# Mixer of a three-block transformer: five more convolution taps on Pool, the forget gates' chain called later in the code, a head's output copied out of PSUM by ScalarE

## The chip, the cores and the metric

The kernel runs on one core of a Trainium2 chip, in one launch. The metric is the device time of an execution in microseconds; the time of the kernel before is the median of three runs, 2093.25 us (2092.4 to 2098.12). One more execution was recorded by the hardware profiler; that one took 2092.26 us.

## The reference, cut to what matters

512 tokens of width 1024 go through two transformer blocks (differential attention, then windowed attention, each with a gated MLP and a gated side input) and then through the block that the change touches, the mixer:

```python
def conformer_conv_branch(a_in, w_dw, b_dw, g_ln, b_ln, w_out):
    a = a_in[..., :CONV_CH] * jax.nn.sigmoid(a_in[..., CONV_CH:])   # 512 channels
    a = causal_depthwise_conv(a, w_dw, b_dw)                        # 31 taps
    a = jax.nn.silu(layernorm(a, g_ln, b_ln))
    return a @ w_out

def forgetting_attention(q, k, v, f_logit, b_forget, g_q, g_k):     # 8 heads of 64
    ...  # rmsnorm of q and k in each head
    log_f = jax.nn.log_sigmoid(f_logit + b_forget)
    c = jnp.cumsum(log_f, axis=1)
    ...  # softmax(q k / 8 + c_i - c_j), causal, times v

proj = rmsnorm(x, g_mix) @ w_in     # a_in, q, k, v, f_logit, gate_a, gate_b
merged = sigmoid(gate_a) * y_conv + sigmoid(gate_b) * (y_attn @ w_attn_out)
x = x + merged @ w_out              # then one more gated MLP
```

## The kernel before, in words

All activations lie feature-major, as tiles of 128 features by 512 tokens. Every matrix product keeps f32 accuracy by splitting both operands into a high and a low part and adding three products (`mm3`, L188 to L190): high by high, high by low, low by high. So each 512 KB block of weights arrives by DMA (`wr`), is cast by ScalarE (`wh`, L157), and its low part is made by VectorE (`wl`, L158). A `dense` output of 128 features costs 24 matmuls of 128x512 (8 weight blocks, three products each).

The mixer (`mix`) has four tiles of 128 convolution channels, m = 0 to 3. `glu(m)` makes the convolution's input `pad` and the running sum `cacc`. `tap(m, j, ...)` adds tap j of tile m. For the tiles 0 and 1 the first `VT[m]` taps run on VectorE, multiply and add in one instruction into `pacc` in PSUM (L918), and the others on Pool: a product `tap` (made by Pool itself while the attention runs, L924, or by ScalarE afterwards, L926) and Pool's add into `cacc` (L927). With VT = (31, 20), tile 0 is all VectorE's, and of tile 1 twenty taps are VectorE's and eleven are Pool's. The tiles 2 and 3 are all Pool's.

The attention: `qk(m)` projects a pair of heads' k and q; `unit_heads` normalises each of the two by `inv_rms`: squares `isq`, high and low part `ish` and `isl` (L416, L417), a sum over each head's 64 rows by two matmuls into `ps_ss` (L418, L419), and from that the factor `iy` (L425). Eight such halves are made, two of them ahead of the heads. `head(hd)` makes `nb` (the row of -c, L1009 and L1011), four score blocks with their softmax, four transposed blocks (`ps_t`, L1039) split into `ah` and `al`, and twelve matmuls into `ps_o` (L188 to L190, of 512, 384, 256 and 128 columns, three each); the last step splits `ps_o` into the high and low output `xq` (L180 on ScalarE, L181 on VectorE). This text calls the part from the transposes on a head's tail. Between the score blocks the other projections (`gens`) and the taps (`taps`) are called.

After the attention come 16 `gate` products `w_g`, with the remaining taps called between the first twelve, then `attn_conv` of `w_ao` over the attention, and `conv_norm`: `cs`, the sum over the four finished tiles (L1100 on Pool, L1101 and L1102 on VectorE), its split `csh`, the mean over channels by `ps_cs` (L1114), the centred squares, the variance (`ps_tm`, `ps_bc`, L217), SiLU, and the split `cxh`, the operand of `w_co`.

Tiles with one tag of one pool form a ring: in the pool `fp` each tag has three buffers unless told otherwise. Tag "A" holds `nb`, `u` (a projection before its normalisation), `ish` and later `cs`; tag "C" holds `isq`, `isl`, `iy`, `tap` and `csh`. A tile that takes a buffer waits for the last reader of the tile that had it before.

The order of the instructions on each engine is not the code's: the tile framework reorders the program as a list scheduler (`schedule_with_timeline_sim=True`), by dependencies, ring buffers and a model of durations, except where `keep` holds the order of the code. So an edit moves instructions at places that the diff doesn't touch.

Of the kernel before, what the change touches and what calls it, by code (L numbers as in the profile page):

```python
# [11 lines left out]
F32 = mybir.dt.float32  # L12
F32R = mybir.dt.float32r
I32 = mybir.dt.int32
AF = mybir.ActivationFunctionType
ALU = mybir.AluOpType
# [3 lines left out]
P = 128  # L20
D = 1024
T = 512
# [23 lines left out]
SSP = (4, 5)  # L46


VT = (31, 20)
TAPS = ((0, 1),) * 5 + ((0, 2),) * 3  # L50
CSTEP = 12

# [39 lines left out]
def build(tc, nc, a, out):  # L92
    c = Ctx()
# [5 lines left out]
    fp = es.enter_context(tc.tile_pool(name="fp", bufs=3))  # L99
# [5 lines left out]
    V, S, G, TE, Q = nc.vector, nc.scalar, nc.gpsimd, nc.tensor, nc.sync  # L105
# [17 lines left out]
    def spc(name, i=0, n=1):  # L123
        o, w = _SP[name]
        return sp[:, o + i : o + i + n]
# [10 lines left out]
    def act(**kw):  # L136

        name = SETS[kw["func"]]
        if aset["name"] != name:
            ld = S.preload_act_table_set(name)  # L140
            if aset["name"] == LNEXP:
                tc.keep_in_program_order(ld)
            for u in aset["users"]:
                tc.add_manual_dep(ld.ins, u, nosync, reason="tables in order")
            aset.update(name=name, load=ld.ins.name, users=[])
        i = S.activation(**kw)  # L146
        tc.add_manual_dep(i.ins, aset["load"], nosync, reason="tables in order")
        aset["users"].append(i.ins.name)
# [29 lines left out]
    def split(hi, lo, src, scale=None):  # L178
        if scale is None:
            S.copy(out=hi, in_=src)  # L180
            V.tensor_tensor(out=lo, in0=src, in1=rd(hi), op=ALU.subtract)  # L181
        else:
            S.activation(out=hi, in_=src, func=AF.Copy, scale=scale)
            V.scalar_tensor_tensor(out=lo, in0=src, scalar=scale, in1=rd(hi), op0=ALU.mult, op1=ALU.subtract)  # L184
# [45 lines left out]
    h = [None] * KD  # L230
# [630 lines left out]
    def mix(nm, nxt):  # L861
# [25 lines left out]
        def glu(m):  # L887
            pad = mp.tile([P, NT - 1 + T], F32, tag="cv", name="pad", bufs=8)
            G.memset(pad[:, 0 : NT - 1], 0.0)
            V.tensor_tensor(out=pad[:, NT - 1 :], in0=dense("w_a", 2 * m, x), in1=nm.rb, op=ALU.mult)  # L890
            pads[m] = pad
            yield
            u = mp.tile([P, T], F32, tag="cv", name="cacc", bufs=8)
            V.tensor_tensor(out=u, in0=dense("w_a", 2 * m + 1, x), in1=nm.rb, op=ALU.mult)
            accs[m] = u
            yield

        def glu_gate(m):
# [3 lines left out]
            V.scalar_tensor_tensor(out=p, in0=u, scalar=1.0, in1=p, op0=ALU.add, op1=ALU.mult)  # L902
            n = VT[m] if m < 2 else 0
            bgv.extend((m, j, V) for j in range(n))
# [41 lines left out]
        V.tensor_tensor(out=lg, in0=psf, in1=nm.rb[0:8, :], op=ALU.mult)  # L946
        fq, y, z, w = (sm.tile([P, 32], F32, tag="f" + n, name="f" + n, bufs=1) for n in "qyzw")
        Q.dma_start(out=fq, in_=lg.rearrange("h (c t) -> h c t", t=32))
        V.tensor_scalar(out=fq, in0=fq, scalar1=spc("bf"), scalar2=None, op0=ALU.add)
        V.scalar_tensor_tensor(out=y, in0=fq, scalar=-1.0, in1=fq, op0=ALU.mult, op1=ALU.min)  # L950
        act(out=y, in_=y, func=AF.Exp)

        V.tensor_scalar(out=z, in0=y, scalar1=2.0, scalar2=None, op0=ALU.add)
        V.reciprocal(out=z, in_=z)
        V.tensor_tensor(out=z, in0=z, in1=y, op=ALU.mult)
        V.tensor_tensor(out=w, in0=z, in1=z, op=ALU.mult)
        V.tensor_scalar(out=y, in0=w, scalar1=2.0 / 17.0, scalar2=2.0 / 15.0, op0=ALU.mult, op1=ALU.add)
        for n in (13, 11, 9, 7, 5, 3, 1):
            V.tensor_tensor(out=y, in0=y, in1=w, op=ALU.mult)
            V.tensor_scalar(out=y, in0=y, scalar1=2.0 / n, scalar2=None, op0=ALU.add)  # L960
        V.tensor_tensor(out=y, in0=y, in1=z, op=ALU.mult)
        V.scalar_tensor_tensor(out=y, in0=fq, scalar=0.0, in1=y, op0=ALU.min, op1=ALU.subtract)
        lf = fp.tile([8, T], F32, tag="B", name="lf", bufs=4)
        Q.dma_start(out=lf.rearrange("h (c t) -> h c t", t=32), in_=y)
        cc = fp.tile([8, T], F32, tag="B", name="cc", bufs=4)
        V.tensor_tensor_scan(out=cc, data0=lf, data1=lf, initial=0.0, op0=ALU.add, op1=ALU.bypass)
        ch = ma.tile([P, T], F32R, name="ch")
        G.memset(ch.bitcast(I32), 0)
        split(ch[0:8], ch[32:40], cc)

        def unit_heads(ps, g, tag, bufs):

# [11 lines left out]
        def qk(m):  # L984

            pk = dense("w_qk2", 2 * m + 1, x)
            hk = unit_heads(pk, gqk[:, 1:2], "hk", 1)
            yield
            pq = dense("w_qk2", 2 * m, x)
            hq = unit_heads(pq, gqk[:, 0:1], "hq", 1)  # L990
            yield
            for j in range(2):
                sl = slice(64 * j, 64 * j + 64)
                q, k, kl = (ma.tile([P, T], F32R, tag="st", name="st", bufs=9) for _ in range(3))
                for b in range(2):
                    o = slice(64 * b, 64 * b + 64)
                    Q.dma_start(out=rd(k[o]), in_=rd(hk[sl, 0]))
                    Q.dma_start(out=rd(q[o]), in_=rd(hq[sl, b]))
                    Q.dma_start(out=rd(kl[o]), in_=rd(hk[sl, 1]))
                sts[2 * m + j] = q, k, kl  # L1000
            yield

        ox = Quads()

        def head(hd):
            q, kh, kl = sts[hd]

            pc = att.tile([P, T], F32, tag="tp", name="ps_c")
            TE.matmul(pc, nid[:, hd : hd + 1].to_broadcast([P, P]), ch, start=True, stop=True)  # L1009
            nb = fp.tile([P, T], F32, tag="A", name="nb")  # L1010
            S.copy(out=nb, in_=pc)  # L1011
            ee = []
            for i in range(4):
                wd = (i + 1) * P
                ps = att.tile([P, T], F32, tag="sc", name="ps_s", bufs=BANKS["sc"])
                scores(ps[:, :wd], q, kh, kl, slice(i * P, wd), slice(0, wd), False)
                TE.matmul(ps[:, i * P : wd], idr, trir, start=False, stop=True)
                mx = sm.tile([P, 1], F32, tag="mx", name="mx")
                su = sm.tile([P, 1], F32, tag="su", name="su")
                if i < 2:  # L1020
                    e = ma.tile([P, 256], F32, tag="e", name="e", bufs=3)
                else:
                    e = fp.tile([P, T], F32, tag="B", name="e", bufs=4)
                V.tensor_tensor_reduce(
                    out=e[:, :wd], in0=ps[:, :wd], in1=nb[:, :wd], scale=1.0, scalar=-3.0e38,
                    op0=ALU.add, op1=ALU.max, accum_out=mx,
                )
                V.tensor_scalar(out=mx, in0=mx, scalar1=-1.0, scalar2=None, op0=ALU.mult)
                act(out=e[:, :wd], in_=e[:, :wd], func=AF.Exp, bias=mx, scale=1.0, accum_out=su)
                V.reciprocal(out=su, in_=su)  # L1030
                V.tensor_scalar(out=e[:, :wd], in0=e[:, :wd], scalar1=su, scalar2=None, op0=ALU.mult)
                ee.append(e)
                yield
            po = att.tile([64, T], F32, tag="po", name="ps_o", bufs=1)
            for kb in range(4):
                wd = T - kb * P
                pt = att.tile([P, T], F32, tag="tp", name="ps_t")
                for i in range(kb, 4):
                    TE.transpose(pt[:, (i - kb) * P : (i - kb + 1) * P], ee[i][:, kb * P : (kb + 1) * P], ident)  # L1039
                ah, al = (ma.tile([P, T], F32R, tag=n, name=n, bufs=2) for n in ("ah", "al"))  # L1040
                split(ah[:, :wd], al[:, :wd], pt[:, :wd])
                vb = tuple(z[:, hd * 64 : hd * 64 + 64] for z in vt[kb])
                mm3(po[:, kb * P :], vb, (ah[:, :wd], al[:, :wd]), kb == 0, kb == 3)
            par = slice((hd % 2) * 64, (hd % 2) * 64 + 64)
            split(*(z[par] for z in ox[hd // 2]), po)
            yield


# [3 lines left out]
        def vproj(hf):  # L1052
            pss = tok_major("w_v2", 2 * hf, x)
            cols = slice(256 * hf, 256 * hf + 256)
            for t in range(4):
                split(vt[t][0][:, cols], vt[t][1][:, cols], pss[t], nm.rt[:, t : t + 1])
            yield

        for _ in chain(qk(0), vproj(0), *(glu(m) for m in (2, 3))):
            pass  # L1060
        for m in (2, 3):
            glu_gate(m)
# [106 lines left out]
        for m in range(KD):  # L1169
            t = ga[m]  # L1170
# [168 lines left out]
```

## Time and profile before

| what | us |
| --- | --- |
| median of three runs | 2093.25 (2092.4 to 2098.12) |
| the profiled execution | 2092.26 |
| its span, first to last instruction | 2090.3 |
| TensorE (PE) busy | 2007.4 |
| VectorE (DVE) busy | 1374.4 |
| ScalarE (ACT) busy | 908.1 |
| Pool busy | 472.4 |

The mean granted clock of TensorE is 0.987 of full speed. The mixer fills about 1301 to 1700 us of the span, its attention about 1400 to 1565, and the taps end at 1631. A busy time counts overlapped matmuls once; a wait is idle time of an engine with the instruction that ended it. PE is TensorE, DVE VectorE, ACT ScalarE.

### The profile page before, as it was taken

The numbers are of one execution on the slowest core, as the hardware profiler recorded it, in microseconds if no ns is written. First come the engines' busy times: TensorE is split into PE (matmuls) and PEld (weight loads), VectorE is DVE, ScalarE is ACT, GpSimd is POOL, SyncE is SP. The second block draws the span as 40 slices with busy tenths as digits, with TensorE's granted clock in tenths as the row PEclk, the third lists the DMA queues.
The fourth block names the chain that finished last, engine by engine and source line by source line (L and its number), as shares of the span: only waits on it lengthen the run. The fifth ranks groups of instructions, "written<-read, shape, count | busy, mean of one in ns | idle before, by whom it ended". The sixth has DMA issues, their size and how long they took to land.

```text
span 2090.3 us, 25027 instructions
## 1 busy us (share of the span) xinstructions
PE 2007.4 (96%) x9374; PEld 1650.3 (79%) x9374; DVE 1374.4 (66%) x2174; ACT 908.1 (43%) x1447; POOL 472.4 (23%) x337
## 2 busy tenths in 40 slices
PE   7999889999999998989999999999999899999999
PEld 6888668888888876768888888778778688888887
DVE  7786858747466756777647467778889765434443
ACT  5465635424244536654324244545556343222221
POOL 2465322000002236530000002305599040000000
PEclk9999999999999999999999999999999999999999
DMA  4643422232223252212222223233222232222222
GB/s 162 170 122 104 149 71 91 81 110 101 92 101 125 106 172 72 81 51 92 89 103 101 93 99 133 75 100 119 86 86 73 79 106 96 93 99 101 91 101 91
DMA packets 69465, 212.43 MB, mean 102 GB/s; under 512 B 9568, under 2 KB 9568, under 8 KB 68832
## 3 DMA queue, kind: packets, MB, share of 16 engines
q1 hardware_dynamic: 69344, 210.84, 30.3%
q8 instruction: 74, 1.21, 0.2%
q14 instruction: 47, 0.39, 0.1%
HBM read 179.31 MB, written 6.29 MB: 89 GB/s over the span
## 4 chain that ended last, share of the span: by engine, by line
PE 78%; DVE 10%; POOL 5%; ACT 3%; issue 2%; DMA 2%; SPq 0%; POOLq 0%; DVEq 0%; ACTq 0%
PE ps_d L188 24%; PE ps_d L190 24%; PE ps_d L189 24%; POOL cacc L927 3%; DVE wl L158 1%; POOL tap L924 1%; DMA wr<-w_qk 1%; PE ps_s L395 1%; PE ps_s L396 1%; PE ps_o L189 1%; PE ps_o L190 1%; ACT e L146 1%; PE ps_o L188 1%; ACT wh L157 1%; DVE xV L184 1%
## 5 line engine op out<-in xcount | busy, mean ns | idle before, releaser
L157 ACT CAST wh<-wr 128x1024 fp32r<-128x1024 f32 (+1 forms) x323 | 337.8, 1048 | 650.3 <-PE ps_d L189 563.5
L188 PE MATMUL ps_d<-xO,wh 128*128 128x512 f32 x1400 | 548.3, 392 | 7.2 <-ACT wh L157 3.3
L190 PE MATMUL ps_d<-xO,wl 128*128 128x512 f32 (+1 forms) x1400 | 547.9, 392 | 3.6 <-DVE wl L158 3.6
L189 PE MATMUL ps_d<-xV,wh 128*128 128x512 f32 (+1 forms) x1400 | 547.0, 391 | 0.0
L158 DVE TENSOR_TENSOR wl<-wr,wh 128x1024 fp32r<-128x1024 f32 x286 | 367.3, 1286 | 83.3 <-ACT wh L157 81.1
L188 PEld LDWEIGHTS ps_d<-xO,wh 128*128 128x128 f32 x1400 | 263.0, 188 | 65.3 <-ACT wh L157 5.4
L190 PEld LDWEIGHTS ps_d<-xO,wl 128*128 128x128 f32 (+1 forms) x1400 | 262.8, 188 | 60.4 <-DVE wl L158 5.3
L189 PEld LDWEIGHTS ps_d<-xV,wh 128*128 128x128 f32 (+1 forms) x1400 | 262.9, 188 | 55.8 <-DVE xV L184 0.6
L271 POOL TENSOR_TENSOR ss<-ss,sq 128x512 f32<-128x512 f32 x44 | 69.6, 1582 | 800.4 <-ACT sq L269 787.8
L314 DVE TENSOR_TENSOR u<-ps_d,rb 128x512 f32<-128x512 f32 x156 | 106.4, 688 | 203.5 <-PE ps_d L190 196.4
L189 PE MATMUL ps_d<-gl,wh 128*128 128x512 f32 x528 | 204.4, 389 | 0.0
L190 PE MATMUL ps_d<-gh,wl 128*128 128x512 f32 x528 | 203.2, 389 | 0.0
L188 PE MATMUL ps_d<-gh,wh 128*128 128x512 f32 x528 | 203.2, 389 | 0.0
L188 PE MATMUL ps_d<-xq,wh 128*128 128x512 f32 x448 | 179.1, 404 | 21.2 <-ACT wh L157 8.7
L190 PE MATMUL ps_d<-xq,wl 128*128 128x512 f32 x448 | 178.6, 399 | 1.4 <-DVE wl L158 1.3
L189 PE MATMUL ps_d<-xq,wh 128*128 128x512 f32 x448 | 178.8, 399 | 0.9 <-DVE xq L184 0.9
L766 DVE TENSOR_TENSOR h<-h,ps_d 128x512 f32<-128x512 f32 x72 | 48.6, 685 | 175.4 <-PE ps_d L190 175.4
L188 PEld LDWEIGHTS ps_d<-xq,wh 128*128 128x128 f32 x448 | 86.3, 193 | 40.9 <-ACT wh L157 9.0
L158 POOL TENSOR_TENSOR wl<-wr,wh 128x1024 fp32r<-128x1024 f32 x37 | 90.5, 2451 | 111.0 <-ACT wh L157 95.7
L189 PEld LDWEIGHTS ps_d<-gl,wh 128*128 128x128 f32 x528 | 99.1, 188 | 20.7
L188 PEld LDWEIGHTS ps_d<-gh,wh 128*128 128x128 f32 x528 | 99.1, 188 | 20.6
L190 PEld LDWEIGHTS ps_d<-gh,wl 128*128 128x128 f32 x528 | 99.2, 188 | 20.4
(317 smaller groups left out, 3127.5 us busy)
## 6 DMA issues: line engine op xcount, KB each, us to landing
wr<-w_up SPq DMA_DIRECT2D x132, 512.0 KB, 3.4
wr<-w_dn SPq DMA_DIRECT2D x66, 512.0 KB, 3.5
wr<-w_qk SPq DMA_DIRECT2D x34, 512.0 KB, 3.5
qst<-rt SPq DMA_DIRECT2D x64, 128.0 KB, 2.7
wr<-w_pg SPq DMA_DIRECT2D x16, 512.0 KB, 3.5
wr<-w_g SPq DMA_DIRECT2D x16, 512.0 KB, 3.4
wr<-w_v SPq DMA_DIRECT2D x14, 512.0 KB, 3.5
st<-qhl SPq DMA_DIRECT2D x48, 128.0 KB, 2.3
```

Of the source, the lines that this page charges most:

```text
L146: i = S.activation(**kw)
L157: S.copy(out=hi, in_=raw)
L158: lo_eng[0].tensor_tensor(out=lo, in0=raw, in1=rd(hi), op=ALU.subtract)
L184: V.scalar_tensor_tensor(out=lo, in0=src, scalar=scale, in1=rd(hi), op0=ALU.mult, op1=ALU.subtract)
L188: TE.matmul(ps, lh, rh, start=start, stop=False)
L189: TE.matmul(ps, lh, rl, start=False, stop=False)
L190: TE.matmul(ps, ll, rh, start=False, stop=stop)
L271: (V if self.first and k not in SSP else G).tensor_tensor(out=self.ss, in0=self.ss, in1=sq, op=ALU.add)
L314: V.tensor_tensor(out=u, in0=ps, in1=rb, op=ALU.mult)
L395: TE.matmul(ps, q[:, qc], k[:, kc], start=True, stop=False)
L766: V.tensor_tensor(out=h[m], in0=h[m], in1=ps, op=ALU.add)
L927: G.tensor_tensor(out=accs[m], in0=accs[m], in1=t, op=ALU.add)
```

## The change

Three edits in `mix`. `VT` goes from (31, 20) to (31, 15), so that tile 1 has five `L918` less on VectorE and five products on ScalarE with five adds on Pool more. The forget gates' chain, from the bias to the split of `ch`, becomes a function that is called behind the first `qk` and `vproj` in the code. And a head's output is copied from PSUM into a tile `ou` by ScalarE, and the split reads `ou`; `ou` is a tile of tag "A", in the ring of three with `nb`, `u` and `ish`.

```diff
-VT = (31, 20)
+VT = (31, 15)
@@
-        V.tensor_scalar(out=fq, in0=fq, scalar1=spc("bf"), scalar2=None, op0=ALU.add)
...
-        split(ch[0:8], ch[32:40], cc)
+
+        def forget():
+
+            V.tensor_scalar(out=fq, in0=fq, scalar1=spc("bf"), scalar2=None, op0=ALU.add)
...
+            split(ch[0:8], ch[32:40], cc)
@@
             par = slice((hd % 2) * 64, (hd % 2) * 64 + 64)
-            split(*(z[par] for z in ox[hd // 2]), po)
+            u = fp.tile([P, T], F32, tag="A", name="ou")[par]
+            S.copy(out=u, in_=po)
+            split(*(z[par] for z in ox[hd // 2]), u)
@@
-        for _ in chain(qk(0), vproj(0), *(glu(m) for m in (2, 3))):
+        for _ in chain(qk(0), vproj(0)):
+            pass
+        forget()
+        for _ in chain(*(glu(m) for m in (2, 3))):
             pass
```

Behind the edits the lines of the changed kernel are counted 3 higher in `head` and 8 higher from the gates on (L1012 for L1009, L1042 for L1039, L1122 for L1114).

ScalarE, around the `ish` of the last of the eight halves. Before, head 3's `ps_o` is cast straight into `xq`, two instructions ahead of the squares:

```order
L146 ACTIVATE e,su<-e,mx 128x512
L183 ACTIVATE qhl<-u,gs 128x512
L180 CAST xq<-ps_o 64x512
L1011 COPY nb<-ps_c 128x512
L413 ACTIVATE isq<-u 128x512
L416 CAST ish<-isq 128x512
L157 CAST wh<-wr 128x1024
```

In the changed kernel:

```order
L180 CAST ah<-ps_t 128x256
L180 CAST ah<-ps_t 128x128
L1049 COPY ou<-ps_o 64x512
L180 CAST xq<-ou 64x512
L413 ACTIVATE isq<-u 128x512
L416 CAST ish<-isq 128x512
L157 CAST wh<-wr 128x1024
L1014 COPY nb<-ps_c 128x512
```

The head is now head 4, one further, and its last transposed blocks, its copy and its cast stand ahead of `ish`. `ish` takes the buffer of tag "A" that `ou` of this head has, and so waits for VectorE's subtraction that reads it. The same holds for three other of the last six halves, behind the heads 0, 1 and 3.

TensorE, at the last half's two sums. Before, they stand between blocks of the convolution's projection and ahead of head 4's first `ps_o`:

```order
L189 MATMUL ps_d<-xV,wh 128x512
L418 MATMUL ps_ss<-ish,blkr 128x512
L395 MATMUL ps_s<-st 128x256
L396 MATMUL ps_s<-st 128x256
L1017 MATMUL ps_s<-trir,idr 128x128
L395 MATMUL ps_s<-st 128x384
L419 MATMUL ps_ss<-isl,blkr 128x512
L396 MATMUL ps_s<-st 128x384
L188 MATMUL ps_o<-ah,xq 64x512
```

In the changed kernel the tail of head 4 stands 23 matmuls of `ps_d` ahead of the first of them; its end is this:

```order
L188 MATMUL ps_o<-ah,xq 64x384
L1042 MATMUL ps_t<-cn,e 128x128
L189 MATMUL ps_o<-al,xq 64x384
L190 MATMUL ps_o<-ah,xq 64x384
L1042 MATMUL ps_t<-cn,e 128x128 x2
L188 MATMUL ps_o<-ah,xq 64x256
L189 MATMUL ps_o<-al,xq 64x256
L190 MATMUL ps_o<-ah,xq 64x256
L188 MATMUL ps_o<-ah,xq 64x128
L1012 MATMUL ps_c<-ch,nid 128x512
L189 MATMUL ps_o<-al,xq 64x128
L190 MATMUL ps_o<-ah,xq 64x128
```

From the mixer's start to the last L419, the changed order has thirty 128x512 matmuls of `ps_d`, the twelve of a head's `ps_o`, one `ps_c` and four `ps_t` more than the order before, and two score blocks (256 and 384 columns) and one 128-column mask less. For the six halves among the heads the whole difference up to their L419 is, in columns of 512, about 0, 32, 23, 16, 7 and 38.

Pool, at the end of the taps. Before:

```order
L924 TENSOR_TENSOR tap<-pad,dwh 128x512
L927 TENSOR_TENSOR cacc<-cacc,tap 128x512 x20
L1100 TENSOR_TENSOR cs<-cacc 128x512
L927 TENSOR_TENSOR cacc<-cacc,tap 128x512 x9
L1100 TENSOR_TENSOR cs<-csq 128x512
```

In the changed kernel:

```order
L924 TENSOR_TENSOR tap<-pad,dwh 128x512
L927 TENSOR_TENSOR cacc<-cacc,tap 128x512 x21
L1108 TENSOR_TENSOR cs<-cacc 128x512
L927 TENSOR_TENSOR cacc<-cacc,tap 128x512 x13
L1108 TENSOR_TENSOR cs<-csq 128x512
```

Five adds more stand ahead of the end. Of the 32 times three matmuls of `w_ao`, 16 single ones stand ahead of `ps_cs` in the changed kernel where 30 did, and 29 instead of 14 between `ps_tm` and `ps_bc`. The products that Pool makes itself (L924) are as many as before, and the first of the last run of them waits for the sixth L419 in both orders. The forget gates' instructions keep their places on every engine: VectorE's order is the same, but for line numbers, far into the attention.

## Rows read from the trace of the kernel before

**Rows 1.** The page: busy time of each engine, share of the span, instructions.

```profile
PE 2007.4 (96%) x9374; PEld 1650.3 (79%) x9374; DVE 1374.4 (66%) x2174; ACT 908.1 (43%) x1447; POOL 472.4 (23%) x337
```

**Rows 2.** What TensorE waited for in 1360 to 1700 us (the mixer): engine, matmul, what ended the wait; us in total, times, longest.

```profile
PE ps_d L188 <- ACT cxh L180: 3.3, 1, 3.3
...
PE ps_cs L1114 <- ACT csh L180: 2.9, 1, 2.9
PE ps_o L189 <- DVE al L181: 2.6, 2, 2.3
```

**Rows 3.** TensorE in order of time at the end of the convolution: start, duration, line, what, and the idle time before it with what ended it. The first two rows are the first and last of 27 matmuls that follow one another.

```profile
1624.61 0.39 PE L188 MATMUL ps_d<-xq,wh 128*128 128x512 f32 x1
...
1630.53 0.39 PE L190 MATMUL ps_d<-xq,wl 128*128 128x512 f32 x1
1633.78 0.50 PE L1114 MATMUL ps_cs<-csh,onesr 128*128 128x512 f32 x1 [2.87 <-ACT csh L180]
...
1653.48 1.10 PE L217 MATMUL ps_bc<-dg,onesr 128*128 128x512 f32 x2 [1.46 <-DVE dg L211]
1657.94 2.93 PE L188 MATMUL ps_d<-cxh,wh 128*128 128x512 f32 x6 [3.35 <-ACT cxh L180]
```

**Rows 4.** VectorE in order of time at the end of the taps, same columns.

```profile
1616.40 2.11 DVE L158 TENSOR_TENSOR wl<-wr,wh 128x1024 fp32r<-128x1024 f32 x1 [1.03 <-ACT wh L157]
...
1619.69 0.69 DVE L1108 TENSOR_TENSOR cacc<-pacc,cacc 128x512 f32<-128x512 f32 x1 [0.51 <-POOL cacc L927]
...
1627.63 1.22 DVE L158 TENSOR_TENSOR wl<-wr,wh 128x1024 fp32r<-128x1024 f32 x1
...
1630.35 0.75 DVE L918 SCALAR_TENSOR_TENSOR cacc<-pad,dwh,pacc 128x512 f32<-128x512 f32 x1
1631.13 0.69 DVE L1101 TENSOR_TENSOR cs<-cacc 128x512 f32<-128x512 f32 x1
```

**Rows 5.** Pool in order of time, from the last L419 of the attention to the last add.

```profile
1515.84 1.04 POOL L924 TENSOR_TENSOR tap<-pad,dwh 128x512 f32<-128x512 f32 x1 [3.66 <-PE ps_ss L419]
...
1521.38 1.95 POOL L924 TENSOR_TENSOR tap<-pad,dwh 128x512 f32<-128x512 f32 x1 [0.63 <-DVE iy L425]
...
1571.80 31.64 POOL L927 TENSOR_TENSOR cacc<-cacc,tap 128x512 f32<-128x512 f32 x20
1603.39 1.30 POOL L1100 TENSOR_TENSOR cs<-cacc 128x512 f32<-128x512 f32 x1
1604.63 15.02 POOL L927 TENSOR_TENSOR cacc<-cacc,tap 128x512 f32<-128x512 f32 x9
```

**Rows 6.** What Pool waited for in 1360 to 1700 us.

```profile
POOL tap L924 <- PE ps_ss L419: 92.1, 6, 59.9
```

**Rows 7.** The first part of Pool's last run as one stretch: us; busy time of PE, PEld, DVE, ACT, POOL with instructions; granted clock of TensorE, DMA share, GB/s.

```profile
1515.84:1571.80 55.96, 51.22 (x254) 40.44 (x253) 46.66 (x96) 28.92 (x62) 53.68 (x42) 0.97 0.26 79
```

**Rows 8.** ScalarE in order of time among the last taps.

```profile
1606.96 0.72 ACT L926 ACTIVATE tap<-pad,dwh 128x512 f32<-128x512 f32 x1 [1.94 <-POOL cacc L927]
...
1608.96 1.03 ACT L157 CAST wh<-wr 128x1024 fp32r<-128x1024 f32 x1
...
1615.34 1.03 ACT L157 CAST wh<-wr 128x1024 fp32r<-128x1024 f32 x1
...
1633.11 0.62 ACT L180 CAST csh<-cs 128x512 fp32r<-128x512 f32 x1
```

**Rows 9.** Groups of one tile's instructions over the whole span, with the shortest, median and longest duration in ns: VectorE's taps, Pool's adds, the same copy as the new one in the second block's attention, and the two ends of the forget gates' chain (its last instruction, and the first matmul that reads it).

```profile
L918 DVE SCALAR_TENSOR_TENSOR pacc<-pad,dwh,pacc x48: 739/743/757, 1569.8 to 1629.6; 128x512 f32<-128x512 f32 x48
...
L927 POOL TENSOR_TENSOR cacc<-cacc,tap x70: 1265/1298/2294, 1424.2 to 1617.5; 128x512 f32<-128x512 f32 x70
...
L687 ACT COPY ou<-ps_o x16: 560/577/579, 788.0 to 917.7; 64x512 f32<-64x512 f32 x16
...
L181 DVE TENSOR_TENSOR ch<-cc,ch x1: 681/681/681, 1397.6 to 1397.6; 8x512 fp32r<-8x512 f32 x1
...
L1009 PE MATMUL ps_c<-ch,nid x8: 396/443/736, 1403.7 to 1532.9; 128*128 128x512 f32 x8
```

**Rows 10.** VectorE's groups in 1410 to 1560 us (the attention): busy us, mean ns; idle before.

```profile
L158 DVE TENSOR_TENSOR wl<-wr,wh 128x1024 fp32r<-128x1024 f32 x18 | 27.4, 1524 | 7.5 <-ACT wh L157 7.4
...
L975 DVE TENSOR_TENSOR u<-u,iy 128x512 f32<-128x512 f32 x6 | 7.4, 1225 | 0.0
...
L181 DVE TENSOR_TENSOR xq<-ps_o,xq 64x512 fp32r<-64x512 f32 x7 | 4.7, 677 | 0.4 <-ACT xq L180 0.3
```

**Rows 11.** Stretches of the attention, the columns of Rows 7.

```profile
1460.00:1480.00 20.00, 20.00 (x104) 16.70 (x102) 16.42 (x34) 11.11 (x21) 6.84 (x6) 1.00 0.31 105
1480.00:1488.00 8.00, 5.80 (x29) 3.99 (x27) 8.00 (x18) 4.55 (x11) 7.76 (x7) 1.00 0.74 193
1488.00:1496.00 8.00, 6.82 (x25) 5.83 (x26) 6.76 (x20) 3.93 (x10) 4.32 (x3) 0.57 0.33 101
1496.00:1520.00 24.00, 23.13 (x118) 18.43 (x117) 20.00 (x41) 14.38 (x30) 14.45 (x12) 1.00 0.18 55
```

**Rows 12.** TensorE in order of time in those stretches, at three places of the heads' tails.

```profile
1489.18 0.47 PE L189 MATMUL ps_o<-al,xq 128*64 128x256 f32 x1 [2.34 <-DVE al L181]
...
1515.36 0.39 PE L419 MATMUL ps_ss<-isl,blkr 128*128 128x512 f32 x1
...
1558.81 0.41 PE L188 MATMUL ps_o<-ah,xq 128*64 128x512 f32 x1 [2.00 <-DVE xq L181]
```

More of the change, by code (lines that the diff above doesn't have):

```diff
@@ L948, in mix @@
         Q.dma_start(out=fq, in_=lg.rearrange("h (c t) -> h c t", t=32))
-        V.tensor_scalar(out=fq, in0=fq, scalar1=spc("bf"), scalar2=None, op0=ALU.add)
[L950 to L963, printed above, removed]
@@ L964, in mix @@
-        Q.dma_start(out=lf.rearrange("h (c t) -> h c t", t=32), in_=y)
-        cc = fp.tile([8, T], F32, tag="B", name="cc", bufs=4)
-        V.tensor_tensor_scan(out=cc, data0=lf, data1=lf, initial=0.0, op0=ALU.add, op1=ALU.bypass)
         ch = ma.tile([P, T], F32R, name="ch")
         G.memset(ch.bitcast(I32), 0)
-        split(ch[0:8], ch[32:40], cc)
+        def forget():
+            V.tensor_scalar(out=fq, in0=fq, scalar1=spc("bf"), scalar2=None, op0=ALU.add)
+            V.scalar_tensor_tensor(out=y, in0=fq, scalar=-1.0, in1=fq, op0=ALU.mult, op1=ALU.min)
+            act(out=y, in_=y, func=AF.Exp)
+            V.tensor_scalar(out=z, in0=y, scalar1=2.0, scalar2=None, op0=ALU.add)
+            V.reciprocal(out=z, in_=z)
+            V.tensor_tensor(out=z, in0=z, in1=y, op=ALU.mult)
+            V.tensor_tensor(out=w, in0=z, in1=z, op=ALU.mult)
+            V.tensor_scalar(out=y, in0=w, scalar1=2.0 / 17.0, scalar2=2.0 / 15.0, op0=ALU.mult, op1=ALU.add)
+            for n in (13, 11, 9, 7, 5, 3, 1):
+                V.tensor_tensor(out=y, in0=y, in1=w, op=ALU.mult)
+                V.tensor_scalar(out=y, in0=y, scalar1=2.0 / n, scalar2=None, op0=ALU.add)
+            V.tensor_tensor(out=y, in0=y, in1=z, op=ALU.mult)
+            V.scalar_tensor_tensor(out=y, in0=fq, scalar=0.0, in1=y, op0=ALU.min, op1=ALU.subtract)
+            lf = fp.tile([8, T], F32, tag="B", name="lf", bufs=4)
+            Q.dma_start(out=lf.rearrange("h (c t) -> h c t", t=32), in_=y)
+            cc = fp.tile([8, T], F32, tag="B", name="cc", bufs=4)
+            V.tensor_tensor_scan(out=cc, data0=lf, data1=lf, initial=0.0, op0=ALU.add, op1=ALU.bypass)
+            split(ch[0:8], ch[32:40], cc)
```

## The prediction

> **What bounds the kernel now.** I read the page first: TensorE is busy 96% of the span [rows 1], so the end moves by what TensorE waits, and a change that moves no matmul's data can only add or remove waits. The waits of TensorE in the mixer come next [rows 2]: no large one, but 3.3, 2.9 and 2.6 us at few places. Two of these, `ps_cs` and `cxh`, lie on one chain, the end of the convolution: TensorE has done its matmuls at 1630.5 + 0.4, and waits for `csh` until 1633.78; from there the layer norm's chain runs to the operand of `w_co` at 1657.94, with TensorE late at its last two steps [rows 3]. So what delays `csh` delays the mixer's end, nearly one for one.
>
> What is `csh` late for? Back in time: VectorE's last tap of tile 0 ends at 1631.1, then L1101, a `ga`, L1102 [rows 4], then the cast [rows 8]. VectorE is the last by a little, not by much: Pool's last add ended at 1619.65, 11.5 us earlier, and VectorE waited 0.51 us for it [rows 4, 5]. The reader should then ask what sets Pool's end. From 1515.84 on Pool hardly waits any more (0.63 us at 1521.38; busy 53.7 of 56.0 us with its 42 starts [rows 5, 7], then adds without a gap); before that it does, and all its waits of size, 92.1 us in six, end with a matmul L419 [rows 6]. The last ends at 1515.84, behind the L419 at 1515.36 [rows 5, 12]. So the last L419 in the attention starts Pool's last run, and the run takes 1619.65 - 1515.84 = 103.8 us.
>
> **The change part by part.**
>
> The forget gates' chain. Its instructions stand where they stood; its last one starts at 1397.6 and its first reader at 1403.7 [rows 9], so 5.4 us of cover lie between. I cost it at 0; if it came later by more than that, each further us would hold back head 0's scores by a us.
>
> Five taps from VectorE. They take away 5 x 0.743 = 3.7 us of VectorE [rows 9] ahead of L1101, which is up to 2.9 us of TensorE's wait. They add five products on ScalarE, 0.72 each [rows 8], and five adds on Pool. The last 29 adds and one L1100 took 31.64 + 1.30 + 15.02 = 47.96 us [rows 5], 1.60 each (1.30 alone, more where VectorE's `wl` runs beside: 2.11 against 1.22 for that, 2.29 the longest add [rows 4, 9]). Five more are 8.0 us. Pool's end becomes 1619.65 + 8.0 = 1627.6 if its run starts when it did. Then follow VectorE's L1108 (0.69), L1101, another instruction, L1102 and the cast: from L1101's start to `ps_cs` it took 1633.78 - 1631.13 = 2.65, so 3.3 us, or 4.5 with a `wl` of 1.22 in between [rows 3, 4]. I take 3.9: `csh` ready for `ps_cs` at 1631.5, which is 2.3 us earlier than before. Alone, this edit gains 2.3 us, and Pool is then the one that is late, with nothing to spare: every us that Pool's run starts later is paid.
>
> The copy `ou`. Eight copies of 0.58 us [rows 9] on ScalarE, busy 11 to 14 of 20 to 24 us in the attention [rows 11]. They lie in a chain, however, `ps_o` to `xq`: between 0 and 8 x 0.58 = 4.6 us, and I take 0 beside the delays below, which hold them. It gives something as well: `ps_o` has one buffer, and is free after the copy instead of after the cast and VectorE's subtraction; at 1558.81 TensorE waited 2.00 us for that [rows 12]. That wait is behind the last L419, and ahead of gates that are paced by Pool, so I count 0 of it (2.0 at most if Pool were early).
>
> VectorE's subtraction of `xq` now reads two operands in SBUF. It took 677 ns from PSUM; u times `iy`, with two in SBUF, took 1225 on average in the same stretch [rows 10]. Eight times 0.55 is 4.4 us of VectorE, some 2.7 of it ahead of the last half. VectorE is busy 16.4 to 20.0 of 20 to 24 us there [rows 11], so this is not hidden by much.
>
> The Trainium skill has a rule against moving work between these two engines: "Perfetto Trace Analysis", section "Optimizing Scalar/DVE Operations", says that GpSimd and VectorE share a read port, so offloading between them might not help. The taps do not bear it out: VectorE's L918 took 739 to 757 ns with Pool busy beside it. By the rule the five taps would bring nothing, and `csh` would come 2.3 us later than I have it.
>
> The ring, which is the largest term. `ou` takes a buffer of `nb`, `u` and `ish`, and the order shows what follows: four of the six halves' `ish` wait for a head's last subtraction, and the tails of the heads stand ahead of them. Up to the last L419 TensorE has the work of 38 matmuls of 512 columns more. 27 of these took 1630.53 - 1624.61 = 5.92 for 26 steps [rows 3], 0.228 each: 8.6 us. All of it is work that TensorE did later in the order before, so it costs TensorE nothing; but Pool's last run starts that much later. Call this delay d. To 8.6 us come the waits in the tails, which now stand with little else between them. Up to 1515 the order before had one bad tail: from 1480 to 1496 TensorE was idle 3.4 us, 2.34 of it for `al`, and the clock fell to a mean of 0.57 for 8 us [rows 11, 12], which at 6.82 busy us loses about 2.9. If the new order keeps none of that, d = 8.6 - 6.3 = 2.3. If it has a second such tail, d = 14.9. VectorE, which has two `wl` (2 x 1.5 [rows 10]), a score block, two `al` and a subtraction more ahead of the last half, besides the 2.7 us above, says about 8 too. I take one short wait more than before: d = 10.
>
> The sum: `ps_cs` at 1631.5 + 10 = 1641.5 against 1633.78, so +7.7. Of the gates, ScalarE's casts `wh` stand in order behind its products, which wait for Pool's adds (1.94 at 1606.96), 6.4 us from one to the next where 24 matmuls take 5.5 [rows 3, 8]; they come later with Pool's run, so TensorE waits between the gates rather than in one piece, with the same total. Behind `ps_cs` the chain of 24.2 us stays; fourteen matmuls of `w_ao` now stand (by the order) behind it instead of ahead, 3.2 us of work which fits into its waits of 1.46 and 3.35 [rows 3], and gives nothing, since the chain ends last. The profiled execution took 2092.3, so the forecast is 2100.0; the median of before is 1.0 above that execution, which lets +6.7 remain against the median. A measurement of this kernel can tell 0.3% from no change, 6.3 us.
>
> **Rivals.**
>
> *The tails lose their waits.* `ps_o` comes free sooner, TensorE's order has the tails packed, and the 6.3 us of 1480 to 1496 vanish: d = 2.3, `ps_cs` at 1633.8, the end at 2092.3: no change. For it: the bad tail is one place, with a new order around it. Against it: what ended its wait was VectorE's `al`, and VectorE has more to do, not less. It decides below d = 8.6, where the result is within 0.3%.
>
> *Pool's run isn't later at all*, since VectorE, with slower instructions on Pool's account, and not TensorE's place sets L419 in both kernels: d = 0, the 2.3 us of the taps stay, and with the wait of 2.0 at 1558.81 gone as far as Pool allows it the end is at 2088 to 2090. For it: VectorE had no idle time at all in 1480 to 1488 [rows 11]. Against it: VectorE's own list up to that half is longer as well. This is the side of faster; over 0.3% would need more than both gains at once.
>
> *The packed tails stall.* With no other matmuls between transposes, `al` and `ps_o`, each tail waits for ScalarE and VectorE in turn, and the clock falls behind it as at 1488. One such tail more is +6.3: d = 15, the end at 2105; two of them 2111.
>
> **How the numbers follow.** The forecast's own case, d from 8.6 to 13, has 0.40 (2098.6 to 2103); the stalled tails 0.13; the lost waits, d from 2 to 8.6, 0.29 (2092 to 2098.6); the start of Pool's run unmoved 0.18, of which half would be over 0.3% faster if the tails also save what stalled before. Slower by over 0.3% from the median is above 2099.5: most of the first case and all of the second, 0.50. Faster 0.09, the same 0.41. The range leaves out the two stalled tails and the lower half of the last case: 2089 to 2107.
>
> **What would show it.** Pool's last wait for an L419 ends d later than 1515.84, 10 us by my sum; behind it Pool runs without idle time for 111 to 112 us instead of 103.8. VectorE's last tap ends ahead of Pool's last add, and L1108 of tile 1 waits for Pool some us instead of 0.51. `ps_cs` waits for `csh` again, at about 1641. The subtraction of `xq` from `ou` takes 1.0 to 1.4 us where Pool is busy. The wait of 2.00 for `xq` at `ps_o` is gone. The forecast is wrong if the last L419 comes at the old time, or if Pool is idle again behind it, or if `ps_cs` isn't late for Pool's end.

## The result, and the profile after

The changed kernel takes 2123.9 us (2122.88 to 2128.22, four runs) against 2093.84 (2092.4 to 2098.12): a ratio of 1.0141, 95% interval 1.0127 to 1.0155. It is slower by 30 us where I had forecast 2100 and a range to 2107. The direction was right, the size was not.

The profiled execution took 2122.88 us, its span is 2120.8, 30.5 more than before. The page's first part, as in [rows 1]:

```profile
PE 2018.4 (95%) x9374; PEld 1654.8 (78%) x9374; DVE 1373.2 (65%) x2169; ACT 918.4 (43%) x1460; POOL 484.4 (23%) x342
```

TensorE has the same 9374 instructions and is busy 11.0 us longer, so it ran slower for a while; the other 19.5 us of the 30.5 are idle. What it waited for in 1410 to 1600 us, the attention (in us: total, times, longest):

```profile
PE ps_t L1042 <- DVE e L1034: 13.6, 7, 3.4
PE ps_o L189 <- DVE al L181: 8.5, 7, 2.8
PE ps_o L188 <- ACT ah L180: 3.5, 6, 1.1
PE ps_d L188 <- DVE cacc L894: 1.8, 1, 1.8
PE ps_s L395 <- DMA st<-qhl: 1.7, 1, 1.7
```

The first three are links of a head's tail: normalised `e`, transposed, split into `ah` and `al`, multiplied. They came to 4.4 us before (`al` 2.6, `e` 1.8) and come to 25.6 now. The same stretches as in [rows 11], ten us each, columns as there; those left out have TensorE busy throughout:

```profile
1424.00:1434.00 10.00, 7.08 (x53) 6.15 (x51) 9.89 (x21) 5.01 (x14) 8.98 (x8) 0.94 0.21 66
1434.00:1444.00 10.00, 8.52 (x51) 7.25 (x52) 4.43 (x12) 2.88 (x8) 1.43 (x1) 0.71 0.06 15
...
1454.00:1464.00 10.00, 6.11 (x29) 4.39 (x27) 9.93 (x14) 5.12 (x11) 9.61 (x7) 0.98 0.31 88
1464.00:1474.00 10.00, 7.84 (x33) 6.42 (x34) 5.98 (x18) 3.46 (x9) 3.34 (x3) 0.68 0.59 149
...
1494.00:1504.00 10.00, 6.29 (x30) 4.71 (x29) 9.90 (x23) 5.17 (x11) 9.14 (x7) 0.86 0.37 89
1504.00:1514.00 10.00, 9.01 (x41) 6.29 (x40) 7.37 (x21) 4.70 (x13) 6.73 (x6) 0.63 0.37 103
...
1524.00:1534.00 10.00, 6.50 (x28) 4.94 (x27) 9.62 (x17) 3.56 (x8) 9.43 (x7) 0.89 0.25 67
1534.00:1544.00 10.00, 9.15 (x43) 6.97 (x42) 2.74 (x5) 3.22 (x6) 0.00 (x0) 0.94 0.28 100
1544.00:1554.00 10.00, 6.44 (x31) 4.94 (x29) 6.48 (x16) 5.79 (x13) 5.42 (x4) 0.92 0.11 27
1554.00:1564.00 10.00, 6.64 (x25) 4.03 (x26) 7.13 (x11) 2.34 (x6) 9.61 (x9) 0.57 0.36 94
```

Five places, each with idle time and, within or behind it, a lower granted clock. A place costs the idle time plus busy time times (1 - clock): 7.3, 8.7, 8.9, 5.6 and 10.3 us in the order of the rows. They sum to 40.8, of which 26.4 are idle time and 14.4 the slower clock. Up to the last L419 the order before had one such place, of 6.3 us, from 1480 to 1496 [rows 11]. The eye should also go to the columns of VectorE and Pool: three of the idle stretches from 1454 on have VectorE busy 9.6 to 9.9 of 10 and Pool 9.1 to 9.6.

One tail, head 0's, in order of time (the first three are TensorE's, from its timeline; start, duration, wait in brackets):

```profile
1432.91 0.69 PE L1042 MATMUL ps_t<-cn,e 128*128 128x128 f32 x2 [2.41 <-DVE e L1034]
1434.06 0.69 PE L188 MATMUL ps_o<-ah,xq 128*64 128x512 f32 x1 [0.46 <-ACT ah L180]
1436.17 0.69 PE L189 MATMUL ps_o<-al,xq 128*64 128x512 f32 x1 [1.42 <-DVE al L181]
```

```profile
1442.59 0.58 ACT L1049 COPY ou<-ps_o 64x512 f32<-64x512 f32 x1 [3.41 <-PE ps_o L190]
1443.21 0.62 ACT L180 CAST xq<-ou 64x512 fp32r<-64x512 f32 x1
...
1443.86 0.68 DVE L181 TENSOR_TENSOR xq<-ou,xq 64x512 fp32r<-64x512 f32 x1 [3.75 <-ACT xq L180]
1445.50 0.62 ACT L416 CAST ish<-isq 128x512 fp32r<-128x512 f32 x1
```

Each link waits for the one ahead, up to 1438 us TensorE has nothing beside it, and `ish` comes behind the subtraction, as the order said. Pool, in order of time, against [rows 5]:

```profile
1451.99 1.04 POOL L924 TENSOR_TENSOR tap<-pad,dwh 128x512 f32<-128x512 f32 x1 [16.56 <-PE ps_s L1020]
...
1478.23 1.04 POOL L924 TENSOR_TENSOR tap<-pad,dwh 128x512 f32<-128x512 f32 x1 [10.81 <-PE ps_ss L419]
...
1548.35 1.04 POOL L924 TENSOR_TENSOR tap<-pad,dwh 128x512 f32<-128x512 f32 x1 [14.61 <-PE ps_ss L419]
...
1604.43 33.84 POOL L927 TENSOR_TENSOR cacc<-cacc,tap 128x512 f32<-128x512 f32 x21
1638.23 1.29 POOL L1108 TENSOR_TENSOR cs<-cacc 128x512 f32<-128x512 f32 x1
1639.48 20.39 POOL L927 TENSOR_TENSOR cacc<-cacc,tap 128x512 f32<-128x512 f32 x13
```

Its last run starts 32.5 us later and takes 1659.87 - 1548.35 = 111.5 us (103.8 before). `ps_cs` comes at 1663.8, 30.0 later, and waits 4.24 us.

Two lengths serve below, each within one execution: **A**, the attention, from the first `ps_c` to the start of the last subtraction into `xq`, and **B**, from there to the first `ps_cs`. Before: A 161.6, B 68.4. Changed: A 193.4, B 65.6. The loss is in A: +31.8. A as one stretch, before and changed, columns as in [rows 7]:

```profile
1403.74:1565.33 161.59, 151.15 (x781) 123.74 (x780) 133.67 (x276) 84.92 (x176) 105.55 (x80) 0.97 0.35 103
1404.80:1598.16 193.36, 162.38 (x781) 128.67 (x780) 132.96 (x276) 91.05 (x182) 108.01 (x80) 0.90 0.30 86
```

TensorE runs the same 781 matmuls, with 31.0 us idle where it had 10.4, and at a lower mean clock.

### The profile page after: what moved, and what is told of

It reads as the page before. It is cut to its first block, busy times and chain, and to the rows that moved or that the text cites. A ratio compares the mean times of both kernels' runs of the same rounds, so it can differ in the third digit from the quotient of the medians.

```text
span 2120.8 us, 25050 instructions
## 1 busy us (share of the span) xinstructions
PE 2018.4 (95%) x9374; PEld 1654.8 (78%) x9374; DVE 1373.2 (65%) x2169; ACT 918.4 (43%) x1460; POOL 484.4 (23%) x342
## 4 chain that ended last, share of the span: by engine, by line
PE 79%; DVE 10%; POOL 5%; ACT 2%; issue 2%; DMA 1%; SPq 1%; DVEq 0%; POOLq 0%; ACTq 0%
PE ps_d L188 24%; PE ps_d L190 24%; PE ps_d L189 24%; POOL cacc L927 4%; POOL tap L924 1%; DVE wl L158 1%; PE ps_s L395 1%; PE ps_s L396 1%; PE ps_o L189 1%; ACT e L146 1%; PE ps_o L190 1%; PE ps_o L188 1%; DVE xV L184 1%; DVE at L181 1%; PE ps_t L493 1%
```

## The experiments

Two theories stood at first: that the ring of tag A, through the order, makes the tails stall; and that the copy with its slower subtraction costs the time wherever it stands. The forget gates' chain got no run of its own: up to 1428 us, which is past that chain and the first `ps_c`, every engine has the same instructions in the same order in the traces of both kernels.

**1. The taps alone**, in the kernel before.

```diff
-VT = (31, 20)
+VT = (31, 15)
```

> The kernel before with VT = (31, 15) alone; the attention's order is that of before. Ring theory (the copy's buffer in tag A puts the heads' tails ahead of the halves' ish and stalls TensorE there, and Pool's last run starts with the last L419): Pool's last run starts at 1515 to 1517 as before, lasts about 111.5 us instead of 103.8, ps_cs at 1631.5, time about 2091 (2089 to 2094). Copy theory (the longer chain ps_o, ou, xq and the slower subtraction cost the time wherever they stand): the same 2091. Tap theory (Pool's five more adds are the loss): 2102 or more.

2090.03 us, ratio 0.9986 (0.9975 to 0.9998): faster by 2.8. A is 161.6 as before, B 66.2. Pool, in order of time:

```profile
1514.80 1.04 POOL L924 TENSOR_TENSOR tap<-pad,dwh 128x512 f32<-128x512 f32 x1 [3.62 <-PE ps_ss L419]
...
1570.71 32.73 POOL L927 TENSOR_TENSOR cacc<-cacc,tap 128x512 f32<-128x512 f32 x21
1603.39 2.29 POOL L1100 TENSOR_TENSOR cs<-cacc 128x512 f32<-128x512 f32 x1
1605.64 20.34 POOL L927 TENSOR_TENSOR cacc<-cacc,tap 128x512 f32<-128x512 f32 x13
```

Pool's last add ends at 1625.98, so the run lasts 1625.98 - 1514.80 = 111.2; the taps' term was sized right, and the tap theory falls.

**2. The copy alone:** the changed kernel with the old taps (the place of `forget` changes nothing).

```diff
-VT = (31, 15)
+VT = (31, 20)
```

> The changed kernel with VT back at (31, 20). Ring and copy theory: the last L419 stays at about 1548 as in the changed kernel (1547.9), Pool's run lasts 103.8 and ends near 1652, VectorE's last tap 3.7 us later than the 1658.2 of the changed kernel, so 2117 to 2126. Tap theory: most of the 30 us comes back, 2094 to 2102.

2123.89 us, 1.0142 (1.0121 to 1.0162). The last L419 at 1550.1, A 195.3. All of the loss is the copy's. That the five taps bring nothing here, where they bring 2.8 without the copy, I had not singled out: TensorE waits only 0.6 us at `ps_cs` in this run, so what it lost in the attention is what is late.

**3 and 4. The copy in another ring**, in the changed kernel: tag B in 3, tag C (with its three buffers) in 4.

```diff
-            u = fp.tile([P, T], F32, tag="A", name="ou")[par]
+            u = fp.tile([P, T], F32, tag="B", name="ou", bufs=4)[par]
```

> The changed kernel with the copy ou in tag B (four buffers, with the softmax's e) instead of A. In its order the first five halves' L419 stand where they stood before, the last 7 us of matmuls later, with no more heads' tails ahead of it than before. Ring theory: no stalls at the first five, the last L419 8 to 14 us later than before, 2099 to 2106. Copy theory: the eight copies and the eight slower subtractions are still there, 2118 to 2126.

> The changed kernel with the copy ou in tag C (three buffers, with isq, isl, iy and Pool's tap). In its order a head's tail stands ahead of five of the six L419 and the second to fifth come 7 to 16 us of matmuls later than before, the last 9.5. Ring theory: as bad as the change or worse, 2118 to 2135, with the second and third L419 later than in the changed kernel. Copy theory: 2118 to 2126 as with every ring.

Tag B: 2100.55 us, 1.0036 (1.0021 to 1.0051), A 170.8. Tag C: 2121.42 us, 1.0139 (1.0114 to 1.0163), A 199.1. The same eight copies cost 10.5 us over the taps alone in one ring and 31 and 34 in the others: so the copy theory, by which the whole loss comes with the copies, falls, and the ring decides over most of it. The subtraction of `xq` is even slower with tag B, 1222 ns on average against 852. The ring acts through the order: `ish` itself waits 0.27 us for the subtraction at the last half of the changed kernel, and no row of `ps_ss` stands among TensorE's waits there. In tag C the loss is of another make: 27 more matmuls stand within A, the three links of the tail come to 13.5 us, and `ps_ss` waits 6.0 for `ish`. Where the 10.5 us with tag B come from isn't shown; runs 7 and 11 bear on it. In detail I was off: with tag B the last L419 comes 144.2 us behind the first of the mixer (139.5 before), 4.7 later and not 8 to 14; with tag C the second comes when it does in the changed kernel.

**5 and 6. How much of the stalls is Pool's doing?** The same two orders, with Pool's taps in the attention cut from 512 to 32 columns, in both lines, so that part of the convolution is left out.

```diff
-                    keep(G.tensor_tensor(out=t, in0=src, in1=w.to_broadcast([P, T]), op=ALU.mult))
+                    keep(G.tensor_tensor(out=t[:, 0:32], in0=src[:, 0:32], in1=w.to_broadcast([P, 32]), op=ALU.mult))
...
-                G.tensor_tensor(out=accs[m], in0=accs[m], in1=t, op=ALU.add)
+                z = slice(0, 32 if alone else T)
+                G.tensor_tensor(out=accs[m][:, z], in0=accs[m][:, z], in1=t[:, z], op=ALU.add)
```

> The changed kernel with Pool's own taps in the attention cut to 32 of 512 columns in both instructions (L924 and their L927), so that part of the convolution is left out; TensorE's order up to the last L419 is the changed kernel's. Contention theory (the tails stall because Pool's bursts behind each L419 stretch VectorE's instructions): VectorE's e<-e,su falls from a mean of 892 to about 500 ns, the waits of ps_t and ps_o in the attention from 25.6 to under 8 us, and the last L419 comes at 1530 or sooner. Order theory (the tail's own chain e, ps_t, ah, al, ps_o has nothing beside it and stalls at any speed of VectorE): the waits stay over 16 us and the last L419 comes after 1540.

> The kernel before with the same cut of Pool's taps in the attention (part of the convolution left out), as control for e5. Both theories: the waits for e, al and ah, 4.4 us before, fall to 0 to 3, the last L419 comes at 1510 to 1515. The end is then no more set by Pool: 2085 to 2092.

2099.32 us, 1.0037 (1.0027 to 1.0047), and 2076.36 us, 0.9925 (0.9898 to 0.9951, two executions). A is 170.5 with the changed order and 149.5 with the one before. So the changed order costs 21.0 us with Pool nearly silent and 31.8 with it (in time 23.0 and 30.1): two thirds are the tails' own chain, a third comes only together with Pool's bursts. Neither theory had it alone. VectorE's group of the normalising step and TensorE's waits in run 5:

```profile
L1035 DVE TENSOR_SCALAR e<-e,su 128x128 f32<-128x128 f32 (+3 forms) x32 | 12.0, 387 | 0.5
```

```profile
PE ps_o L189 <- DVE al L181: 4.6, 6, 2.1
PE ps_t L1043 <- DVE e L1035: 3.9, 3, 2.3
PE ps_o L188 <- ACT ah L180: 3.4, 6, 0.9
```

The step took 892 ns on average in the changed kernel, 387 here; but it took 908 in the kernel before, so the change did not make it slower; what the order of the change takes away is the other work that TensorE had beside it. The waits for `e` fall from 13.6 to 3.9; those for `al` and `ah` less. The three waits sum to 11.9, between the two expectations; the last L419 comes at 1529.9, as the contention theory had it. The control missed its time: 2076.36 where I had 2085 to 2092, since Pool's taps slow VectorE in the order before as well (A falls by 12.1, and the step on `e` from 908 to 386 ns).

**7 and 8. The copy for the last heads only:** the kernel before with VT = (31, 15) and this, from head 5 in 7, from head 4 in 8.

```diff
-            split(*(z[par] for z in ox[hd // 2]), po)
+            u = po
+            if hd >= 5:
+                u = fp.tile([P, T], F32, tag="A", name="ou")[par]
+                S.copy(out=u, in_=po)
+            split(*(z[par] for z in ox[hd // 2]), u)
```

> The kernel before with VT = (31, 15) and the copy ou in tag A for the heads 5 to 7 alone, which are behind the last half; order up to the last L419 as before. Ring theory: the last L419 at 1515, the time of e1 (2090, 2087 to 2093), the wait of 2.0 for xq at ps_o gone or smaller. Copy theory: three eighths of the loss, some 10 us above e1.

> The same with the copy from head 4 on: the first five halves stand as before, the last L419 stands 9.5 us of matmuls later, behind the tail of head 4. Ring theory: last L419 at 1528 to 1532 (9.5 and one tail's stalls of 3 to 7), Pool's last run behind it, 2102 to 2107. Copy theory: 2106 to 2110 (half the loss), with the last L419 earlier than 1528.

From head 5: 2093.21 us, 1.0003 (0.9992 to 1.0013), A 159.7. That is 3.2 us above run 1 and just outside the range (ten executions each, 2091.0 to 2098.4 here and 2088.1 to 2094.8 there), though TensorE and Pool have the order of run 1 throughout. The wait of 2.0 at `ps_o` is gone and A is 1.9 shorter; B is 68.4, 2.2 longer. So the three copies cost nothing in A; the 3 us lie elsewhere and have no cause shown, and the copy theory had 10. From head 4: 2105.57 us, 1.0073 (1.0051 to 1.0095), A 173.4. One more copy, and with it one half behind a tail, costs 12 us:

```profile
1529.45 1.68 POOL L924 TENSOR_TENSOR tap<-pad,dwh 128x512 f32<-128x512 f32 x1 [18.72 <-PE ps_ss L419]
```

That is 14.7 us behind the 1514.80 of run 1, 13.9 when the first wait of Pool is laid on the same time: 9.5 of work moved ahead and some 4.4 of stalls. Here one tail was well priced.

**9. The slower subtraction**, in the changed kernel.

```diff
-            split(*(z[par] for z in ox[hd // 2]), u)
+            hi, lo = (z[par] for z in ox[hd // 2])
+            S.copy(out=hi, in_=u)
+            V.tensor_tensor(out=lo, in0=po, in1=rd(hi), op=ALU.subtract)
```

> The changed kernel with the high part cast from ou and the subtraction reading ps_o in PSUM (so it takes 0.68 us beside Pool, and ps_o is held as long as before). If the slower subtraction has a share in the stalls, the stretch from the first to the last L419, 172.5 us in the changed kernel and 139.5 before, falls by more than 3 us. If only the places in the order count: 169 to 177, 2118 to 2128.

One time of 2123.35 us; 1549.63 - 1378.25 = 171.4 us from the first to the last L419, and A 193.3. The subtraction has no share that shows.

**10 and 11. Does Pool's wait carry the loss to the end?** Pool's own products take buffers of tag B, so they don't share with `isl`: in 10 in the changed kernel, in 11 in the kernel before with VT = (31, 15).

```diff
-                t = fp.tile([P, T], F32, tag="C", name="tap")
+                t = fp.tile([P, T], F32, tag="B", name="tap", bufs=4) if alone else fp.tile([P, T], F32, tag="C", name="tap")
```

> The changed kernel with Pool's own products (L924) in tag B instead of C, so that they no longer share buffers with isl and do not wait for L419; the halves stand in TensorE's order as in the changed kernel. If Pool's wait for the last L419 is what carries the stalls to the end: Pool is not idle for an L419, ps_cs comes less than 110 us behind the last L419 (115.9 in the changed kernel), 2100 to 2115. If the stalls of TensorE set the end by themselves: 2118 or more with the old distance.

> The kernel before with VT = (31, 15) and Pool's own products in tag B. Pool no longer waits for L419 (32 us in five waits in e1), so its last add comes 5 us or more ahead of 1626 and VectorE's taps are last; ps_cs up to 3 us earlier than in e1: 2085 to 2090. If the spread of Pool's work over the whole attention slows VectorE there as much as the bursts do: 2088 to 2094.

Run 10: 2116.8 us, 1.0113 (1.0089 to 1.0136, two executions). Pool waits no more for an L419, and `ps_cs` still comes 115.7 us behind the last one; A is 189.2, and Pool now waits for ScalarE's first product, which stands behind the attention:

```profile
1594.87 31.68 POOL L927 TENSOR_TENSOR cacc<-cacc,tap 128x512 f32<-128x512 f32 x20 [12.05 <-ACT tap L926]
```

So neither expectation holds whole: without Pool's wait for L419 24 of the 30 us stay, but another wait of Pool has come in its place, and the run alone doesn't part Pool's share from TensorE's. Run 11: 2097.19 us, 1.0012 (1.0001 to 1.0023), A 168.7, 7.2 us worse than run 1 and outside both ranges: Pool now waits 42.8 us for transposed blocks (`ps_t`) instead of L419. With no copy at all, a new tenant of tag B costs 7 us here, so with tag B in run 3 too the sharing may be what costs.

**12. Between the two.** The kernel before with 16 taps.

> The kernel before with VT = (31, 16). Pool's last add 1.6 us earlier than in e1, VectorE's last tap 0.74 later; both end within a us of each other: 2089 to 2092, like e1.

2090.61 us, 0.9988 (0.9978 to 0.9997): the same as run 1. These two, without the copy, are faster than the kernel before by 0.1%.

## Why the prediction was wrong

*What holds.* The forget gates' chain costs nothing. The taps: Pool's run of 111.5 us was forecast as 111.8, `ps_cs` in run 1 is 2.3 us earlier after the start of the attention (227.8 against 230.0), as forecast. The ring that the copy shares is the cause of most of the loss, shown by runs 3, 7 and 8, and in the changed kernel the last L419 does start Pool's last run.

*The step that failed is d.* I wrote "I take one short wait more than before: d = 10". Measured: 1548.35 - 1515.84 = 32.5. The 8.6 us of work moved ahead in it stand as counted from the order; the stalls, for which I took 1.4, are 24. One stalled place had been sized about right, 6.3 against 5.6 to 10.3, but I added no whole one: up to the last L419 four stand where one stood (30.5 us against 6.3), and a fifth behind it. With 32.5 for d the sum gives `ps_cs` at 1664.0, and it came at 1663.8, so no other term of the sum was off by much. The rival of the packed tails named the mechanism and got a chance of 0.13, and its second step, "two of them 2111", fell outside the range. I had the evidence to count them: the order shows a tail without filler ahead of four of the halves, and the trace had one such tail with its price.

*The carrier was wrong too.* I held that the moved work "costs TensorE nothing" and only Pool's later start is paid. For the work that is so, but stalls are time TensorE itself loses: 19.5 us idle and 11.0 us of slower running are the 30.5 of the span. Between the gates, where I had placed the waits for Pool, there are none. From the end of A to shortly ahead of `ps_cs` TensorE is busy throughout at the full clock:

```profile
1598.16:1659.50 61.34, 61.34 (x271) 50.48 (x269) 57.09 (x68) 42.17 (x62) 58.83 (x40) 1.00 0.24 78
```

Only the wait of 4.2 us at `ps_cs` can be the price of Pool's late end, and it was 2.9 before. TensorE and Pool were late by about the same, which let a sum over Pool alone come out right with the measured d. Run 2 agrees: its last run on Pool is 8 us shorter (VectorE has the five taps instead), TensorE waits 0.6 at `ps_cs`, and the time is the same.

*The rule that I weighed*, of the Trainium skill's "Perfetto Trace Analysis", section "Optimizing Scalar/DVE Operations", said that work moved between VectorE and GpSimd might gain nothing. For the taps run 1 says otherwise, 2.8 us. But Pool's slowing of VectorE belongs to the third of the loss that I left out, on other instructions: VectorE's step on `e`, with all operands in SBUF, took 892 ns on average with Pool's bursts and 387 without, while L918, with `pacc` in PSUM, took 746 (741 to 756) beside Pool. The Trainium skill, "SBUF — State Buffer", section "Who interferes with whom", says that VectorE contends with a GpSimd instruction that reads SBUF where it has two inputs there or runs in a two-port mode; these rows agree, if the step on `e` is in such a mode. No row says so outright; in run 5 it takes 284 ns for 128 columns and 492 for 512, 0.54 per column, where the split into `al` takes 288 and 683, 1.03 per column.

*Other steps:* VectorE's subtraction of `xq` took 852 ns on average, less than the 1.0 to 1.4 us expected, and run 9 finds no cost in it. L1116, L1108 before, waited 1.09 us for Pool's last add (0.51 before), so Pool was the later of the two, as forecast, by little.

*Open:* which link of the tail the 21 us without Pool's bursts fall to, and whether a ring of its own for `ou` would be free of them; no run has that ring. Of the 34 us that the copies cost over run 1, about 10 stay with tag B; the 3.2 us of three copies in run 7 leave room for a cost of the copies themselves, and run 11 for one of sharing tag B. The split into two thirds and one third rests on one profile of each kernel.

## What to carry to other kernels

A new tile in a shared ring is an edge in the scheduler's graph: look first at what the ring's other tiles wait for afterwards, since eight copies of 0.6 us cost 34 us in one ring and 10 in another, and three of them 3 where no half stood behind them. In a changed order, count the places where a chain across engines has lost the independent work beside it, and price each from the one that the old trace shows, the slower clock behind it included. And before the loss is put down to the engine that waits visibly, ask what the busy engine itself lost.

## What the runs showed of the hardware

An idle stretch of TensorE costs more than its length: in the five places it was idle for 26.4 us, and the lower granted clock took another 14.4 of its busy time. At 1554 to 1564 us, behind and between such stretches, the mean granted clock was 0.57, between its two levels of 1.2 and 2.4 GHz. And VectorE's step on `e` takes 2.3 times as long on average with Pool's bursts (387 to 892 ns), more than the 1.8 that the two rows of before on the subtraction give (677 and 1225), while the split into `al`, which reads PSUM, takes 678 and 683 ns for 512 columns with and without them.
